# Reordered tokens in the slot strings of a causal convolution's product loop

## The chip, the cores and the metric

The kernel runs on one core of a Trainium2 chip. The metric is the device time of one execution in microseconds (us), the median over runs. The trace that goes with it is one profiled execution of the same program. The engines are called by the short names of the trace: PE (TensorE, matrix products), DVE (VectorE), ACT (ScalarE), POOL (GpSimd) and SP (SyncE, which here only issues transfers).

## The reference

```python
x:      (B=8, S=4096, D=512) float32
kernel: (K=8, 512, 512) float32
for k in range(8):
    shifted = x moved k places later along S (zeros come in, per batch)
    out += shifted @ kernel[k]
```

Each output row is the sum of eight products: the row itself and its seven predecessors, each with a 512x512 matrix of its own.

## The kernel before, in words

**Layout.** The 8 x 4096 rows are cut into 128 runs of 256 consecutive rows. One "time" t of all 128 runs is a block of 128 rows x 512. In `XR`, a ring of 20 such blocks in bf16, each block lies transposed (features on the partitions), so that it can be the stationary operand of a product. One `product` (line 116) is four matmuls, one for each 128 of the 512 features, accumulated into one PSUM bank of 128x512 float32.

**Fewer products.** The eight taps are split three times in two. At each split the kernel takes a sum or a difference of input blocks and of matrices, and so gets by with fewer products than the eight of the reference. Matrix sums are made once, at the start, into the tiles `W[a, b, c]`. Input sums are made all the time on DVE: `z` (line 137, differences or sums of blocks of `XR` into `Z`), `s` (line 151, pairs of `Z` into one of the two `S` tiles), `A` (line 148, pairs of `Z` into one of the two `A` tiles), and `F` in two halves (`node_F`, line 154: `F0` fills blocks 0 and 1 of the single tile `F`, `F1` blocks 2 and 3).

**Nodes and slots.** After a start that handles the first 16 times of each run (nodes 0 to 5, lines 331 to 561), 20 rounds follow, each for 12 new times. A round has four nodes, in the order PL, MI, H1, H0. The loop at line 569 handles one node for each pass, a slot. In a slot three nodes are worked on at once: `cur` gets its last products, `nxt` its middle ones, and `two` (two nodes ahead) has its input sums made. The string `SLOT[cur.a]` names the steps in the order in which they are issued. An engine carries out its own steps in that order; between engines only data dependencies count. This is all that sets the order: it is written by hand, and no planner moves anything.

The steps of a slot, each with its engine:

- `l00 l01 l10 l11`: products of `cur` (PE, line 210), one each into the four banks `p[b][:, j]`; they read block `2b+j` of `F`. For H0 each is two products that read `S`.
- `a1`/`b1`, `a0`, `u`: the products in the bank pair `q` of the node (PE, lines 164 to 182), with a copy by ACT between `a1` and the other two (lines 169, 172). `a1` and `a0` read `A`, `u` reads `Z`.
- `s0`, `s1`, `dt`: ACT copies that seed the bank pairs `p[0]`, `p[1]` of `nxt` from `q`, and the tile `DT` (lines 184, 192).
- `v0`, `v1`: products into `p[b][:, 1]` (PE). `d0`, `d1`: DVE makes `p[b][:, 0]` from `DT` and `p[b][:, 1]` (lines 205, 207). H0 has neither.
- `e0`, `e1`: the finished pair `p[b]` is taken out (line 233): by ACT for PL, by DVE for MI, H1 and H0; H1 and H0 then issue a store on SP. `g0`, `g1` (line 261): one more DVE combination each, and a store.
- `x`: SP issues DMA transposes of new blocks into `XR`, two in a PL slot and one in an MI slot, none in the others. They overwrite blocks that `z` has read.
- `r`: POOL copies two elements of `A` (line 107, so that it waits for `A`), then issues three loads of rows far ahead.

A step whose node lacks it issues nothing (`F`, `v`, `d`, `dt` of an H0 node).

The three bank pairs `pp0` to `pp2` go round from node to node; the fourth, `pp3`, is `q` of every node. So a seed waits until the pair's former node has been taken out.

Of the kernel before, what the change touches and what calls it, by code (L numbers as in the profile page):

```python
# [9 lines left out]
H1, H0, MI, PL = 0, 1, 2, 3  # L10
# [4 lines left out]
def kernel(  # L15
# [317 lines left out]
    for k in range(6):  # L333
# [227 lines left out]
    node_d(n6, 1)  # L561
    later = {6: ((H1, LO, MID),), 7: ((H1, HI, MID),)}
    SLOT = {
        PL: "s l00 F1 a0 l01 u l11 e0 s0 s1 dt F0 z x A v0 d0 v1 d1 l10 a1 e1",
        MI: "l00 s F1 a0 l01 u l11 e0 s0 s1 dt F0 z x A v0 d0 v1 d1 l10 a1 e1",
        H1: "l00 s F1 a0 l01 u l11 e0 s0 s1 dt F0 z A r g0 v0 d0 v1 d1 l10 e1",
        H0: "l00 s F1 b1 l01 a0 u l11 e0 s0 s1 dt F0 z x A g1 v0 d0 v1 d1 l10 a1 e1",
    }
    for k in range(6, len(nodes)):
        cur = nodes[k]  # L570
# [66 lines left out]
```

## Time and profile before

| | |
|---|---|
| runs | 759.54 us median of 3 (757.14 to 759.89) |
| profiled execution | 759.61 us, span 757.9 us |
| PE busy | 733.4 us of the span |
| DVE busy | 692.0 us of the span |
| ACT, POOL busy | 255.0, 62.1 us |
| start until 103 us | PE busy 9.43 of the first 15.40, 49.15 of the next 50.90, 28.02 of the next 36.70 |
| 103 to 133 us | PE busy 29.61, DVE busy 29.79 of 30.00 |
| 133 to 753 us | PE busy 616.87, DVE busy 595.06 of 620.00 |

The profiled execution's own time stands within 0.1 us of the median. Stamps below are us from the start of the span. A line of the timeline gives start, duration, engine, source line and operation, output and inputs, how many such instructions follow one another, and in brackets how long the engine had been idle and for whom it waited. The duration of a matmul reaches past the start of the next, since they overlap; the distance of starts is what one costs. The loop's first slot (PL) starts at 99.69 us on PE, and its first round ends at 133.19 us. All DVE additions and subtractions are issued from the one helper line L82; they are told apart by their tiles.

### The profile page before, as it was taken

To read this page: it belongs to the slowest core of one execution; us is meant where nothing else is said; L and a number is where in the kernel's file an instruction comes from. 1 tells how busy PE (TensorE), PEld (TensorE's weight loads), DVE (VectorE), ACT (ScalarE), POOL (GpSimd) and SP (SyncE) were. 2 spreads that over 40 slices of the span, in tenths; PEclk is the share of its full clock that TensorE was granted. 3 is DMA by queue.
4 is the path that set the end of the run, shared out by engine and by line. 5 is a ranking of instruction groups with operands and counts; after the bars stand their busy time and mean duration, and the time that the engine had idled before them with its cause. 6 is when DMAs were issued, how large, how long until landed. Compare 5 with 4: busy or idle time off the path is not lost.

```text
span 757.9 us, 8920 instructions
## 1 busy us (share of the span) xinstructions
PE 733.4 (97%) x3352; PEld 330.7 (44%) x3420; DVE 692.0 (91%) x727; ACT 255.0 (34%) x380; POOL 62.1 (8%) x103
## 2 busy tenths in 40 slices
PE   6999689999999999999999999999999999999997
PEld 2544234444444444444444444444444444444443
DVE  1774899999999999999999999999999999999996
ACT  4264332333333233333323333332423323232331
POOL 5020201010010101001010110101011010100000
PEclk9999899999999999999999999999999999999999
DMA  9979798877969688696977859597885958784424
GB/s 206 206 141 162 195 252 173 212 193 168 236 143 232 163 199 210 151 253 135 228 174 183 240 141 245 136 225 179 185 232 140 250 138 224 182 179 166 139 85 167
DMA packets 159948, 141.51 MB, mean 187 GB/s; under 512 B 130208, under 2 KB 134304, under 8 KB 159776
## 3 DMA queue, kind: packets, MB, share of 16 engines
q1 hardware_dynamic: 145456, 99.89, 47.0%
q0 software_dynamic: 14304, 40.77, 29.7%
q8 instruction: 27, 0.44, 0.2%
q10 hardware_dynamic: 144, 0.26, 0.1%
q14 instruction: 17, 0.14, 0.1%
HBM read 77.33 MB, written 98.57 MB: 232 GB/s over the span
## 4 chain that ended last, share of the span: by engine, by line
PE 88%; DVE 5%; DMA 4%; issue 1%; ACT 1%; POOL 0%; DVEq 0%; ACTq 0%; POOLq 0%
PE pp L118 87%; DMA w<-in_kernel_dram 2%; DMA out_dram<-w 1%; DMA XR<-xd 1%; DVE y L82 1%; DVE Z L82 1%; DVE S L82 1%; DVE w L82 1%; PE pp L295 0%; DVE F L82 0%; DVE pp L207 0%; PE pp L300 0%; DVE y L247 0%; DVE pp L82 0%; ACT pp L188 0%
## 5 line engine op out<-in xcount | busy, mean ns | idle before, releaser
L118 PE MATMUL pp<-w,S 128*128 128x512 bf16 x1114 | 261.6, 381 | 5.7 <-ACT pp L190 3.9
L118 PE MATMUL pp<-w,F 128*128 128x512 bf16 x973 | 248.4, 379 | 2.9 <-DVE pp L82 1.6
L118 PE MATMUL pp<-w,A 128*128 128x512 bf16 x668 | 173.1, 380 | 3.3 <-ACT pp L169 0.7
L118 PEld LDWEIGHTS <-S 128*128 128x128 bf16 x1136 | 111.1, 98 | 140.9 <-issue 9.5
L82 DVE TENSOR_TENSOR Z<-XR 128x3584 bf16<-128x3584 bf16 (+2 forms) x104 | 147.2, 1434 | 4.1 <-DMA XR<-xd 4.1
L118 PEld LDWEIGHTS <-F 128*128 128x128 bf16 x992 | 96.8, 98 | 119.4 <-issue 1.9
L82 DVE TENSOR_TENSOR S<-Z 128x2560 bf16<-128x2560 bf16 x80 | 118.6, 1483 | 0.0
L188 ACT COPY pp<-pp 128x1024 f32<-128x1024 f32 (+1 forms) x85 | 58.7, 691 | 157.6 <-PE pp L118 154.7
L118 PEld LDWEIGHTS <-A 128*128 128x128 bf16 x680 | 65.3, 98 | 87.2 <-DVE A L82 6.2
L172 ACT COPY pp<-pp 128x512 f32<-128x512 f32 x62 | 35.3, 570 | 201.6 <-PE pp L118 201.6
L118 PE MATMUL pp<-w,Z 128*128 128x512 bf16 x378 | 96.8, 379 | 1.1 <-DVE w L82 0.6
L82 DVE TENSOR_TENSOR F<-S 128x1024 bf16<-128x1024 bf16 x124 | 83.2, 684 | 0.0
L247 DVE SCALAR_TENSOR_TENSOR y<-pp,y 128x1024 f32<-128x1024 f32 x40 | 48.8, 1220 | 18.2 <-PE pp L118 17.2
L107 POOL COPY junk<-A 128x2 bf16<-128x2 bf16 x19 | 18.6, 979 | 540.9 <-DVE A L82 540.9
L190 ACT ACTIVATE pp<-pp 128x1024 f32<-128x1024 f32 (+1 forms) x85 | 59.5, 700 | 5.0 <-DVE y L82 3.8
L82 DVE TENSOR_TENSOR A<-Z 128x1024 bf16<-128x1024 bf16 x80 | 55.4, 692 | 3.9
L118 PEld LDWEIGHTS <-Z 128*128 128x128 bf16 x388 | 37.9, 98 | 46.5 <-issue 0.9
L82 DVE TENSOR_TENSOR y<-y,pp 128x1024 f32<-128x1024 f32 (+1 forms) x46 | 54.5, 1190 | 1.5 <-PE pp L118 1.5
L244 ACT ACTIVATE y<-pp 128x1024 f32<-128x1024 f32 x40 | 41.2, 1029 | 42.1 <-PE pp L118 42.1
L82 DVE TENSOR_TENSOR y<-pp,y 128x1024 f32<-128x1024 f32 x40 | 48.7, 1218 | 2.0 <-DMA out_dram<-y 2.0
L262 DVE SCALAR_TENSOR_TENSOR y<-y 128x1024 f32<-128x1024 f32 x40 | 48.7, 1218 | 0.0
L207 DVE SCALAR_TENSOR_TENSOR pp<-pp,DT 128x512 f32<-128x512 f32 x62 | 43.0, 693 | 2.8 <-PE pp L118 2.8
(53 smaller groups left out, 279.1 us busy)
## 6 DMA issues: line engine op xcount, KB each, us to landing
out_dram<-y SPq DMA_DIRECT2D x124, 512.0 KB, 7.8
xd<-in_x_dram POOLq DMA_DIRECT2D x60, 512.0 KB, 10.7
w<-in_kernel_dram POOLq DMA_DIRECT2D x8, 512.0 KB, 20.8
w<-w POOLq DMA_DIRECT2D x5, 512.0 KB, 6.8
w<-in_x_dram POOLq DMA_DIRECT2D x4, 512.0 KB, 11.7
out_dram<-w SPq DMA_DIRECT2D x3, 512.0 KB, 6.7
w<-in_x_dram SPq DMA_DIRECT2D x1, 1024.0 KB, 4.8
XR<-xd SPq DMA_TRANSPOSE x60, 5.1
```

What stands on the lines that cost most here:

```text
L82: nc.vector.tensor_tensor(out=o, in0=a, in1=b, op=op)
L107: nc.gpsimd.tensor_copy(out=junk, in_=z[:, 0:2])
L118: nc.tensor.matmul(bank, lhsT=comp[:, c * P:(c + 1) * P], rhs=w[:, c, :], start=start and c == 0, stop=c == DC - 1, skip_group_check=True)
L172: nc.scalar.copy(out=n.q[:, 0], in_=n.q[:, 1])
L188: nc.scalar.copy(out=o, in_=q)
L190: nc.scalar.mul(out=o, in_=q, mul=-1.0)
L207: nc.vector.scalar_tensor_tensor(out=p[:, 0], in0=p[:, 1], scalar=-1.0, in1=DT, op0=MUL, op1=SUB)
L244: nc.scalar.mul(out=cc[b_], in_=p, mul=0.5)
L247: nc.vector.scalar_tensor_tensor(out=dd[b_], in0=p, scalar=-0.5, in1=cc[b_], op0=MUL, op1=ADD)
L262: nc.vector.scalar_tensor_tensor(out=cc[b_], in0=cc[b_], scalar=2.0, in1=dd[b_], op0=MUL, op1=SUB)
```

## The change

Only the four strings change:

```diff
     SLOT = {
-        PL: "s l00 F1 a0 l01 u l11 e0 s0 s1 dt F0 z x A v0 d0 v1 d1 l10 a1 e1",
-        MI: "l00 s F1 a0 l01 u l11 e0 s0 s1 dt F0 z x A v0 d0 v1 d1 l10 a1 e1",
-        H1: "l00 s F1 a0 l01 u l11 e0 s0 s1 dt F0 z A r g0 v0 d0 v1 d1 l10 e1",
-        H0: "l00 s F1 b1 l01 a0 u l11 e0 s0 s1 dt F0 z x A g1 v0 d0 v1 d1 l10 a1 e1",
+        PL: "s l00 F1 a0 l01 u l11 e0 s0 z s1 v0 F0 A x dt d0 v1 d1 l10 a1 e1",
+        MI: "s l01 l00 F1 a0 u l11 e0 s0 z s1 dt A F0 v0 x v1 d1 l10 d0 e1 a1",
+        H1: "s l00 F1 a0 l01 u l11 s0 dt e0 z s1 A F0 g0 v0 d0 r v1 d1 l10 e1",
+        H0: "s l00 F1 b1 l01 a0 u e0 l11 s0 z s1 dt F0 A v0 x d0 g1 v1 d1 l10 a1 e1",
     }
```

No step is added or dropped, and no operand changes. What moves, read engine by engine (a step that issues nothing is left out):

| slot | engine | before | after |
|---|---|---|---|
| PL | DVE | s F1 F0 z A d0 d1 | s F1 z F0 A d0 d1 |
| MI | PE | l00 a0 l01 u l11 v0 v1 l10 a1 | l01 l00 a0 u l11 v0 v1 l10 a1 |
| MI | DVE | s F1 e0 F0 z A d0 d1 e1 | s F1 e0 z A F0 d1 d0 e1 |
| H1 | DVE | s F1 e0 z A g0 e1 | s F1 e0 z A g0 e1 |
| H0 | DVE | s e0 F0 z A g1 d0 d1 e1 | s e0 z F0 A d0 g1 d1 e1 |

PE's order in the other three slots, and the orders of ACT, SP and POOL in all four, are the same in both kernels: the second seed, `dt`, `x` and `r` move only past steps of other engines.

## The prediction

> **What bounds the kernel now.** I read the busy times first, then the chain that ended last.
>
> ```profile
> PE 733.4 (97%) x3352; PEld 330.7 (44%) x3420; DVE 692.0 (91%) x727; ACT 255.0 (34%) x380; POOL 62.1 (8%) x103
> ```
>
> PE and DVE are both nearly full, so either could bind. The chain in order of time (start, duration, what) tells when:
>
> ```profile
> 122.07 0.70 DVE A L82
> 122.82 2.78 PE pp L118 x12
> ...
> 133.19 10.79 PE pp L118 x49
> 143.98 0.05 issue
> 144.03 10.78 PE pp L118 x49
> ```
>
> Up to the first round of the loop the chain runs through DVE; from 133 us on it is PE alone, matmul after matmul, until 753 us. A round is 152 matmuls and 32.90 us (l00 of PL starts at 133.19 and, nine rounds later, at 429.33): 20 rounds. Within one steady round, the four slots PL, MI, H1, H0 (each engine's busy us, then granted clock, DMA share, GB/s):
>
> ```profile
> 396.43:404.22 7.79, 7.74 (x36) 3.48 (x36) 7.69 (x9) 3.09 (x5) 0.00 (x0) 1.00 1.01 300
> 404.22:412.01 7.79, 7.79 (x37) 3.51 (x36) 6.73 (x9) 3.09 (x5) 0.00 (x0) 1.00 0.71 138
> 412.01:417.22 5.21, 5.16 (x25) 2.34 (x24) 5.21 (x6) 2.11 (x3) 0.00 (x0) 1.00 0.44 105
> 417.22:429.33 12.11, 12.06 (x57) 5.41 (x56) 12.04 (x14) 2.54 (x5) 2.52 (x4) 1.00 0.80 196
> ```
>
> The third number group is DVE: full but for 1.06 us in MI. So PE binds, DVE has one gap for each round, and what DVE makes arrives shortly before PE needs it. The MI slot shows the gap:
>
> ```profile
> 404.22 1.03 PE L118 MATMUL pp<-w,F 128*128 128x512 bf16 x4
> 405.10 1.02 PE L118 MATMUL pp<-w,A 128*128 128x512 bf16 x4
> 405.96 1.03 PE L118 MATMUL pp<-w,F 128*128 128x512 bf16 x4
> 406.82 1.03 PE L118 MATMUL pp<-w,Z 128*128 128x512 bf16 x4
> 407.02 1.23 DVE L247 SCALAR_TENSOR_TENSOR y<-pp,y 128x1024 f32<-128x1024 f32 x1 [1.02 <-PE pp L118]
> 410.29 1.03 PE L118 MATMUL pp<-w,F 128*128 128x512 bf16 x4
> 410.63 0.69 DVE L82 TENSOR_TENSOR pp<-DT,pp 128x512 f32<-128x512 f32 x1
> 411.22 0.69 DVE L207 SCALAR_TENSOR_TENSOR pp<-pp,DT 128x512 f32<-128x512 f32 x1
> 412.01 1.03 PE L118 MATMUL pp<-w,F 128*128 128x512 bf16 x4
> ```
>
> That is l00, a0, l01, u, then e0 (which waits for l01, 0.20 after u starts), l10, d0, d1, and l00 of H1, which needs d0.
>
> **The change part by part.** Nothing is added or removed; every instruction keeps its duration. The question is only which arrival becomes late for PE, or early enough to remove a wait.
>
> *MI, a0 behind both l's.* a0 waits for the ACT copy behind a1 (404.48 for 0.57, so 405.05). The step from l00 to a0 is 0.88 us, the others 0.86. With l01 in between, the copy has 0.86 more: 0.02 x 20 rounds = 0.4 us less. The bounds are 0 and, by two-digit stamps, 0.03 x 20 = 0.6. H1 keeps l00 a0 (412.01 to 412.90, 0.89) and its wait.
>
> *MI, e0.* Both l's are done one product earlier: e0 can start at 405.96 + 0.20 = 406.16, not 407.02. DVE then has s and F1 done (405.92), so most of the 1.02 gap closes, and z, A, F0 follow by their spacings (1.13, 1.25, 0.61, 0.60) until 409.75.
>
> *MI, d1 before d0.* This opens a new wait. d1 needs v1, the product just ahead of l10. How long after l10's start? e0 gives 0.20; nearer is another d1 that waited for its v1, at the start:
>
> ```profile
> 67.82 1.89 PE L118 MATMUL pp<-w,S 128*128 128x512 bf16 x8
> 68.96 0.70 DVE L207 SCALAR_TENSOR_TENSOR pp<-pp,DT 128x512 f32<-128x512 f32 x1 [2.77 <-PE pp L118]
> ```
>
> Eight matmuls are v1 and v0; v0 starts 0.86 in, at 68.68, and d1 0.28 later. I take 0.28, the same operation: d1 at 410.57, d0 at 411.17, done at 411.86. PE waited for d0 once at the start (done 99.64, matmul 99.69), so 0.05 more: 411.91, against 412.01. The margin falls from 0.64 to 0.10 (0.18 with 0.20). Cost nothing, by that margin; each 0.1 us beyond it costs 20 x 0.1 = 2 us. Behind d0 on DVE stand e1 (411.77, before 411.82), s of H0, F1, e0 of H1 (414.90; it needs l01, 414.63 + 0.20), z and A of PL, done by 418.85 instead of 418.90. PE's b1 needs that A at 418.96, the tightest arrival of the round, and it gains 0.05.
>
> *PL and H0, z before F0.* F0 ends some 2 us later: in PL at 402.1, for l01 of MI at 404.22; in H0 at about 426.1, for l00 of PL at 429.33. Covered by 2.1 and 3.2 us. z and A were neighbours, and A starts 0.03 to 0.10 after z ends (z 399.99 for 2.02, A 402.11), while unrelated neighbours start 0.08 before the end. F0 in between takes that out: 0.11 to 0.18 of DVE in each of the two slots. In steady rounds PE does not notice.
>
> [...]
>
> *H0, d0 before g1.* d0 comes 1.4 us earlier, v0 permitting (v1 starts at 425.88, so from 426.16); l00 of PL had 0.5 us left and has more. g1 and its store come 0.6 later; on SP only e1's store stands behind it, two us away.
>
> *First round, where DVE binds.* PE waits there once for A of PL (0.16 at 122.82). d0 of MI in its new place: z to F0 to A of PL gains 0.18, so d1 starts at 114.37 and d0 ends at 115.66 against 115.24; l00 of H1 wanted 115.54 and starts at 115.71, 0.17 late. But A of PL, DVE 0.18 ahead, ends at 122.58 instead of 122.76, and PE, 0.17 late, arrives at 122.66: in all 0.16 earlier.
>
> *SP, POOL, ACT.* Transposes in PL start 0.6 earlier with z (402.03 before, landing 6.1 later, read at 416.09), the one in MI up to 1.4 earlier; the next store on SP is at 416.20. POOL waits for the same A as before. ACT's seeds wait for u, unmoved; s1 of H1 waits for e0, now earlier.
>
> Sum: -0.4 - 0.16 = -0.56. On the profiled execution, 759.61 (1.7 around the 757.9 span), that is 759.05; its own time is 0.07 above the median of the runs, so I say 759.0. No measurement here tells changes under 0.5% (3.8 us, 0.19 a round) from none.
>
> **Rivals.**
>
> *d0 becomes the bound (slower).* If d1 is released by the end of the next product, l10, and not of v1, it starts at 411.15 + 0.28 = 411.43 and d0 reaches PE at 412.77, 0.76 late: 20 x 0.76 = 15 us, 774. Against it: 68.96, where d1 went while v0 ran. For it: nothing but the thin margin. It decides from 0.10 + 0.19 = 0.29 us of extra delay in each round.
>
> *A smaller form of it.* PE loads weights ahead of a matmul, at 411.80 here. If d0 had to be there for the load, it is 0.11 late, 2.2 us: 761; with a release worse by another 0.1, 763.2. Against it: at 97.67 a load ran two us ahead of the matmul that waited until 99.69.
>
> *PE gets denser (faster).* In the row of 24 matmuls of the H0 slot (423.29 to 428.46) one costs 0.2154; 152 of them are 32.74, 0.16 less than the round. If earlier arrivals removed all of that, 19 x 0.16 = 3.1 us: 755.9. Against it: the other products keep their 0.86 where nothing is late. For more there is no idle time on PE.
>
> The Trainium skill, "TensorE: Matmul & The Clock Gate", section "Back-to-back issue gap", gives about 131 ns for a matmul of 512 columns in a sustained stream. The trace has 0.2165 us. By the page PE would need 20 us a round, DVE with 31.7 would bind, and its savings of up to 0.36 a round would come out as 20 x 0.36 = 7.2 us, 752.3.
>
> **How the numbers follow.** Forecast (no new wait, 758.3 to 759.9): 0.64. Denser PE: 0.14, of which about half beyond 3.8 us, if the runs fall on the low side like 757.14. Small wait: 0.08. d0 bound: 0.11. Unseen others: 0.03. So faster 0.07, same 0.79, slower 0.14. The range takes in the denser PE below (755.9) and the small wait above (763.2); it leaves out the d0 bound and a part of the denser PE.
>
> **What the new profile would show.** In MI, L247's first wait shrinks from 1.02 to about 0.2 and a wait of about 0.8 appears ahead of L207 (d1). Right: round of 32.9 us, l00 of H1 0.86 after a1, a0 of MI no more than 0.87 after its neighbour. Wrong: PE waits named for DVE pp at l00 of H1, 20 times; or a round clearly off 32.9 us.

## The result and the profile after

| | before | after |
|---|---|---|
| runs beside each other (6 each) | 758.92 us median (757.14 to 759.89) | 756.76 us (755.24 to 759.11) |
| ratio | | 0.9979, 95% interval 0.9955 to 1.0003 |
| once more (23 and 12 runs) | 758.45 us (755.27 to 760.16) | 757.57 us (754.77 to 759.43) |
| ratio | | 0.9990, 0.9970 to 1.0009 |
| span of the profiled execution | 757.9 us | 757.3 us |

Both intervals contain 1: the runs do not tell the two kernels apart. The two profiled executions do. Both reach the loop's first product at the same stamp (99.69 and 99.70 us), so their stamps can be compared directly.

The page after (busy us, share of the span, instructions):

```profile
PE 733.1 (97%) x3352; PEld 331.8 (44%) x3420; DVE 690.1 (91%) x727; ACT 254.9 (34%) x380; POOL 62.0 (8%) x103
```

The same work, on the same engines. The chain that ended last, after:

```profile
102.77 0.61 DVE F L82
103.39 0.05 issue
103.43 7.73 PE pp L118 x35
111.16 0.05 issue
111.21 10.91 PE pp L118 x49
122.12 0.05 issue
122.17 10.77 PE pp L118 x49
```

It turns from DVE to PE at 103 us, not only at 133. The wait of b1 for A is nearly gone: b1 starts 1.74 us after l00 of H0 (120.88 to 122.62), where the kernel before has 2.06 (120.76 to 122.82) and a steady round 1.73. The chain hides one wait of that round, because the duration of the product ahead reaches past it: l00 of H1 waits for d0 and starts at 115.70, 1.02 after a1 (114.68) instead of 0.86. The four slots of one steady round after, in the columns shown for before:

```profile
396.08:403.90 7.82, 7.77 (x37) 3.49 (x37) 7.82 (x9) 3.09 (x5) 0.00 (x0) 1.00 1.16 300
403.90:411.68 7.78, 7.78 (x38) 3.52 (x37) 6.50 (x9) 3.09 (x5) 0.00 (x0) 1.00 0.89 165
411.68:416.88 5.20, 5.15 (x24) 2.34 (x24) 5.20 (x6) 2.11 (x3) 0.00 (x0) 1.00 0.24 62
416.88:428.97 12.09, 12.04 (x57) 5.45 (x56) 12.06 (x14) 2.55 (x5) 2.52 (x4) 1.00 0.81 194
```

The round is 32.89 us instead of 32.90. DVE's gap in MI is 1.28 instead of 1.06, and PE is as full as before. The MI slot of that round, PE and DVE:

```profile
403.90 1.89 PE L118 MATMUL pp<-w,F 128*128 128x512 bf16 x8
405.62 1.03 PE L118 MATMUL pp<-w,A 128*128 128x512 bf16 x4
405.82 1.23 DVE L247 SCALAR_TENSOR_TENSOR y<-pp,y 128x1024 f32<-128x1024 f32 x1 [0.54 <-PE pp L118]
...
409.95 1.03 PE L118 MATMUL pp<-w,F 128*128 128x512 bf16 x4
410.22 0.70 DVE L207 SCALAR_TENSOR_TENSOR pp<-pp,DT 128x512 f32<-128x512 f32 x1 [0.71 <-PE pp L118]
410.81 1.03 PE L118 MATMUL pp<-w,Z 128*128 128x512 bf16 x4
410.83 0.69 DVE L82 TENSOR_TENSOR pp<-DT,pp 128x512 f32<-128x512 f32 x1
411.42 1.22 DVE L247 SCALAR_TENSOR_TENSOR y<-pp,y 128x1024 f32<-128x1024 f32 x1
411.68 0.59 PE L118 MATMUL pp<-w,F 128*128 128x512 bf16 x2
```

The new wait of d1 for v1 is there (0.71). d1 starts 0.27 after l10 does (410.22 - 409.95), d0 ends at 411.52, and l00 of H1 starts at 411.68, 0.87 after a1: d0 is in time, by about 0.1 us.

### The profile page after: what moved, and what is told of

Its sections match the earlier page's. It is cut to its first block, busy times and chain, and to the rows that moved or that the text cites. A ratio compares the mean times of both kernels' runs of the same rounds, so it can differ in the third digit from the quotient of the medians.

```text
span 757.3 us, 8900 instructions
## 1 busy us (share of the span) xinstructions
PE 733.1 (97%) x3352; PEld 331.8 (44%) x3420; DVE 690.1 (91%) x727; ACT 254.9 (34%) x380; POOL 62.0 (8%) x103
## 4 chain that ended last, share of the span: by engine, by line
PE 91%; DMA 4%; DVE 2%; issue 1%; ACT 0%; POOL 0%; DVEq 0%; ACTq 0%; POOLq 0%
PE pp L118 91%; DMA w<-in_kernel_dram 2%; DMA out_dram<-w 1%; DMA XR<-xd 1%; DVE y L82 1%; DVE w L82 1%; PE pp L295 0%; DVE S L82 0%; PE pp L300 0%; ACT pp L188 0%; DVE Z L82 0%; DVE F L82 0%; ACT pp L169 0%; ACT pp L190 0%; DVE pp L82 0%
## 5 line engine op out<-in xcount | busy, mean ns | idle before, releaser
L118 PE MATMUL pp<-w,F 128*128 128x512 bf16 x973 | 245.3, 379 | 2.9 <-DVE pp L82 1.7
```

Source lines behind the costliest of these rows:

```text
L118: nc.tensor.matmul(bank, lhsT=comp[:, c * P:(c + 1) * P], rhs=w[:, c, :], start=start and c == 0, stop=c == DC - 1, skip_group_check=True)
```

## A measure that leaves the start out

The runs of one kernel spread over some 5 us, ten times what is at stake. The profiled executions show where most of that lies, ahead of the loop: its first product starts anywhere from 95.80 to 99.83 us, in kernels whose code up to there is the same. So each kernel is read by two numbers that do not contain the start: the time from the loop's first product to the start of the last group on DVE (e1 of the last H0 slot), and the length of a steady round, the distance of the same product row over 15 to 18 rounds. "Alone" means that only this part of the change was made, in the kernel before.

| kernel | loop starts | last DVE group | between | steady round |
|---|---|---|---|---|
| before | 99.69 | 753.42 | 653.73 | 32.904 |
| after | 99.70 | 752.91 | 653.21 | 32.886 |
| after, second execution | 97.46 | 750.76 | 653.30 | 32.89 |
| PE's order in MI alone | 99.69 | 753.08 | 653.39 | 32.885 |
| z and A earlier alone | 97.70 | 751.26 | 653.56 | 32.905 |
| d1 ahead of d0 alone | 95.80 | 749.54 | 653.74 | 32.905 |
| F0 between d1 and d0 | 97.70 | 761.15 | 663.45 | 33.41 |
| d0 behind e1 | 99.83 | 776.71 | 676.88 | 34.07 |
| a0 ahead of both l's | 97.54 | 768.25 | 670.71 | 33.771 |
| swap in PL and H1 too | 97.35 | 749.24 | 651.89 | 32.816 |

The two executions of the changed kernel differ by 0.09 us in this measure and by 0.004 in the round, so it tells some tenths of a microsecond, and not hundredths. The three kernels with one part alone, the one with d0 behind e1 and the one with a0 ahead were each executed once. The whole times of the three are 759.27, 757.46 and 755.75 us in the order of the table, beside 757.13 for one execution of the kernel before; they follow the loop's start (99.69, 97.70 and 95.80) and say nothing of the parts.

## The experiments

**The changed kernel again**, no edit.

> The changed kernel once more, beside the kernel before on the same chip. Theory 1 (PE arrivals: the round is 32.887 us instead of 32.904, and the first round 0.2 us shorter; nothing else differs): 0.55 us below the kernel before, ratio 0.9993, in the profile and in the runs; the further 1.6 us by which the medians of the result differ come from the granted clock of the single runs. Theory 2 (the freed wait of DVE lets something outside the rounds end earlier too): 2.2 us below, ratio 0.9971.

Measured: ratio 0.9990 (0.9970 to 1.0009). From the loop's start, 653.30 us: 0.43 below the kernel before, where the first execution had 0.52. Theory 1 holds for what the loop does. Its last clause, that the granted clock of the single runs makes the rest, is not shown; the last section takes it up. The interval still reaches to 0.9971, so the runs alone do not exclude theory 2; the loop's time does not show a gain of 2.2, and neither does the end (the last product, then DVE, is the same in both).

**PE's order in MI alone.**

```diff
-        MI: "l00 s F1 a0 l01 u l11 e0 s0 s1 dt F0 z x A v0 d0 v1 d1 l10 a1 e1",
+        MI: "l01 l00 s F1 a0 u l11 e0 s0 s1 dt F0 z x A v0 d0 v1 d1 l10 a1 e1",
```

> The kernel before with the new order of PE in MI alone (l01 l00 a0 u). Theory 1 (the shorter round comes from a0, which no longer waits for ACT's copy): round 32.887 instead of 32.904, 19 or 20 x 0.017 = 0.3 us less; the first wait of e0 in MI falls from 1.02 to some 0.2. Theory 2 (it comes from the order on DVE): round stays 32.904.

Measured: round 32.885, 0.34 us less from the loop's start. The whole shortening of the round comes from this part, but only about half of it is the wait of a0 that theory 1 names. In the kernel before, the rounds are not alike: of the 18 behind the first, seven take 32.915 to 32.920 us and eleven 32.893 to 32.897 (l00 of H1 starts at 379.12, 412.01 and 444.93). Here all 18 take 32.884 to 32.887. The seven are the rounds in which the blocks for z of PL wrap round the ring `XR`, so that z is two instructions. In the kernel before, z, A and then b1, first in a short round and then in a long one:

```profile
383.20 2.02 DVE L82 TENSOR_TENSOR Z<-XR 128x3584 bf16<-128x3584 bf16 x1
385.25 0.69 DVE L82 TENSOR_TENSOR A<-Z 128x1024 bf16<-128x1024 bf16 x1
386.05 1.03 PE L118 MATMUL pp<-w,A 128*128 128x512 bf16 x4
...
416.09 2.08 DVE L82 TENSOR_TENSOR Z<-XR 128x1536 bf16<-128x1536 bf16 x2
418.21 0.69 DVE L82 TENSOR_TENSOR A<-Z 128x1024 bf16<-128x1024 bf16 x1
418.96 1.04 PE L118 MATMUL pp<-w,A 128*128 128x512 bf16 x4
```

A ends 0.11 us before b1 starts in the short round and 0.06 before it in the long one. 0.06 is also the distance in the first round, where PE waited for A (122.76 to 122.82), so in the long rounds b1 is late and waits for DVE. With l01 ahead, e0 in MI starts about a product earlier, A of PL comes 0.12 earlier against PE, and that wait is gone. Counted by rounds, the seven waits of 0.024 are about 0.16 us, and a0 gives about 0.009 a round, 0.16 us in all. The smaller figure is only twice the 0.004 by which the two executions of the changed kernel differ.

**z and A earlier alone** (and nothing else).

```diff
-        PL: "... s0 s1 dt F0 z x A v0 d0 ...",
+        PL: "... s0 s1 dt z F0 x A v0 d0 ...",
-        MI: "... s0 s1 dt F0 z x A v0 d0 ...",
+        MI: "... s0 s1 dt z x A F0 v0 d0 ...",
-        H0: "... s0 s1 dt F0 z x A g1 ...",
+        H0: "... s0 s1 dt z F0 x A g1 ...",
```

> The kernel before with z and A ahead of F0 on DVE in PL, MI and H0 as in the changed kernel (PL and H0: z F0 A; MI: z A F0), PE's order and d0, d1, g1 as before. Theory 1: in the first round A of PL comes 0.18 earlier, at 122.64 for b1 instead of 122.82, and PE, not held up by d0, is 0.18 ahead from there on; the round stays 32.904; in all -0.2 us. Theory 2 (DVE pays a pipeline flush after every operation whatever stands next): A of PL at 122.82 as before, 0.

Measured: round 32.905, 0.17 us less from the loop's start. In the first round, l00 of H0 and then b1 on PE:

```profile
118.75 1.89 PE L118 MATMUL pp<-w,S 128*128 128x512 bf16 x7
120.63 1.04 PE L118 MATMUL pp<-w,A 128*128 128x512 bf16 x4
```

1.88 us lie between the two, where the kernel before has 2.06 (120.76 to 122.82). A of PL comes 0.18 sooner, once, as theory 1 has it.

**d1 ahead of d0 alone.**

```diff
-        MI: "... A v0 d0 v1 d1 l10 a1 e1",
+        MI: "... A v0 v1 d1 l10 d0 a1 e1",
```

> The kernel before with d1 ahead of d0 in MI alone. Theory 1: first round l00 of H1 0.35 late (115.89 instead of 115.54), of which 0.02 is left at b1 (DVE is late there anyway); steady rounds d0 ends at 411.92 and reaches PE at 411.97, against 412.01: no wait, round 32.904. So 0. Theory 2 (the wait for v1 comes later than taken, or d0 has to be there for the weight load 0.21 ahead of the matmul): 0.05 to 0.2 in each round, 1 to 4 us.

Measured: round 32.905, 0.01 us more from the loop's start. In the first round PE waits for d0, here with its line:

```profile
112.00 1.02 PE L118 MATMUL pp<-w,F 128*128 128x512 bf16 x4 [0.18 <-DVE pp L82]
```

This row starts 1.21 after the product before it (110.79) instead of 0.86, so l00 is 0.35 late; a part of that is not counted as idle because a matmul's duration reaches past the next start. At b1 the loss is gone, since A is late there anyway. The forecast loss and its return are both there.

**The margin of d0, first step: F0 between d1 and d0.** Edit on the changed kernel:

```diff
-        MI: "s l01 l00 F1 a0 u l11 e0 s0 z s1 dt A F0 v0 x v1 d1 l10 d0 e1 a1",
+        MI: "s l01 l00 F1 a0 u l11 e0 s0 z s1 dt A v0 x v1 d1 F0 l10 d0 e1 a1",
```

> The changed kernel with F0 of MI moved between d1 and d0, so that d0 stands 0.60 us later on DVE. Theory 1 (d0 releases l00 of H1 and its margin is 0.11: done 411.52 in the changed profile, 0.05 to the matmul, which starts at 411.68): l00 of H1 is 0.49 late in each round, 20 x 0.49 = 9.8 us, about 768. Theory 2 (d0 stands off PE's path, or PE has room elsewhere in the round to make it up): no change.

Measured: 768.15 us, ratio to the kernel before 1.0137 (1.0109 to 1.0164); from the loop's start 10.24 us more than the changed kernel. A steady round on PE, a1, l00 of H1, and further on l00 of H0 and b1:

```profile
413.34 1.03 PE L118 MATMUL pp<-w,Z 128*128 128x512 bf16 x4
414.70 1.02 PE L118 MATMUL pp<-w,F 128*128 128x512 bf16 x4 [0.33 <-DVE pp L82]
...
419.87 1.89 PE L118 MATMUL pp<-w,S 128*128 128x512 bf16 x8
421.69 1.04 PE L118 MATMUL pp<-w,A 128*128 128x512 bf16 x4
```

l00 starts 1.36 after a1 instead of 0.87, 0.49 late. That is the 0.60 by which d0 was pushed back, less a margin of 0.11. A second, smaller loss was not forecast: b1 is 0.09 late here (1.82 instead of 1.73), because A of PL stands behind d0 on DVE. This is one of the long rounds, in which z is two instructions; in the others b1 is 0.02 late, some 0.05 in the mean. A third entry gives back 0.03: a0 of H1, which follows l00, has no wait left. Together about 0.51 a round, where the rounds differ by 0.52 (33.41 - 32.89).

**The margin, second step: d0 behind e1.** On the changed kernel:

```diff
-        MI: "... v0 x v1 d1 l10 d0 e1 a1",
+        MI: "... v0 x v1 d1 l10 e1 d0 a1",
```

> The changed kernel with d0 of MI moved behind e1. e1 needs l10, so it starts 0.20 after a1's first matmul (410.81, so 411.01), d0 1.14 later at 412.15, done at 412.84, and l00 of H1 at 412.89 instead of 411.68. Theory 1: 1.21 us late in each round, 20 x 1.21 = 24 us, about 783. Theory 2 (d0 off the path): no change.

Measured, in one execution: 782.91 us; from the loop's start 23.67 us more than the changed kernel, 1.19 a round. A steady round, e1, d0 and l00 of H1:

```profile
421.75 1.23 DVE L247 SCALAR_TENSOR_TENSOR y<-pp,y 128x1024 f32<-128x1024 f32 x1
422.89 0.69 DVE L82 TENSOR_TENSOR pp<-DT,pp 128x512 f32<-128x512 f32 x1
423.63 1.02 PE L118 MATMUL pp<-w,F 128*128 128x512 bf16 x4 [1.05 <-DVE pp L82]
```

d0 ends at 423.58 and the matmul starts 0.05 later. Theory 2 of both steps falls: but for the 0.03 at a0 of H1, the round has no room that makes up for a late d0.

**a0 ahead of both l's.** On the kernel before:

```diff
-        MI: "l00 s F1 a0 l01 u ...",
+        MI: "s a0 l00 F1 l01 u ...",
```

> The kernel before with a0 of MI ahead of l00 too, so that no product stands between a1 and a0. Theory 1 (a0 is paced by ACT's copy behind a1, which reaches PE 0.88 us after the next product could start; one product between them costs 0.86 and so hides all but 0.02, two hide it whole): l00 comes 0.88 late, the round is 32.90 - 0.02 + 0.88 = 33.76, 20 x 0.86 = 17 us more, about 776. Theory 2 (the 0.88 is how these two products are spaced, and no wait): round 32.90.

Measured, in one execution: 774.45 us, round 33.771, 16.98 us more from the loop's start. a1 and a0 of that round:

```profile
408.65 1.03 PE L118 MATMUL pp<-w,A 128*128 128x512 bf16 x4
410.39 1.02 PE L118 MATMUL pp<-w,A 128*128 128x512 bf16 x4 [0.71 <-ACT pp L172]
```

From the start of a1 to the start of a0 at least 1.74 us pass, by way of ACT. One product between them takes the step to 0.86 + 0.88 = 1.74 as well, so it did not hide the copy whole. Two hide it with room: in the changed kernel a0 starts 2.59 after a1 (403.03 to 405.62). That is the wait taken as 0.02.

**The swap in PL and H1 too.** On the changed kernel:

```diff
-        PL: "s l00 F1 a0 l01 u l11 ...",
+        PL: "s l01 l00 F1 a0 u l11 ...",
-        H1: "s l00 F1 a0 l01 u l11 ...",
+        H1: "s l01 l00 F1 a0 u l11 ...",
```

> The changed kernel, and PL and H1 too issue l01 l00 a0 u instead of l00 a0 l01 u. Theory 1 (a0 waits some 0.02 to 0.03 us for ACT's copy wherever only one product stands between a1 and a0; in PL the copy-out e0 on ACT also holds up the seed for v0 by 0.03): H1 gains 0.03, PL 0.01 at a0 and 0.03 at v0, so the round falls from 32.887 to 32.82, 20 x 0.07 = 1.4 us less than the changed kernel. Theory 2 (the 0.88 steps are how matmuls are spaced and no wait): no change against the changed kernel.

Measured: 754.67 us median of 12 runs (753.42 to 756.66), ratio to the kernel before 0.9962 (0.9946 to 0.9979); round 32.816, 1.32 us less than the changed kernel from the loop's start. PL of one round, from l01 and l00 to v0 and v1:

```profile
426.00 1.89 PE L118 MATMUL pp<-w,F 128*128 128x512 bf16 x8
427.72 1.03 PE L118 MATMUL pp<-w,A 128*128 128x512 bf16 x4
428.58 1.03 PE L118 MATMUL pp<-w,Z 128*128 128x512 bf16 x4
429.45 1.03 PE L118 MATMUL pp<-w,F 128*128 128x512 bf16 x4
430.31 1.89 PE L118 MATMUL pp<-w,S 128*128 128x512 bf16 x8
```

and the same stretch of the kernel before, from u on:

```profile
431.93 1.03 PE L118 MATMUL pp<-w,Z 128*128 128x512 bf16 x4
432.79 1.03 PE L118 MATMUL pp<-w,F 128*128 128x512 bf16 x4
433.69 1.02 PE L118 MATMUL pp<-w,S 128*128 128x512 bf16 x4
```

l11 to v0 is 0.86 instead of 0.90: ACT takes out e0 a product earlier and is free when the seed for v0 can be made (e0 at 427.92, the seed at 429.65 after 0.70 of idle time; before, e0 at 432.13 and the seed at 433.05 right behind it). This is the one kernel here whose interval lies wholly below 1, and by the loop's time it beats both the kernel before and the changed one. The loop accounts for 1.84 us of the 3.8 by which its runs lie below the kernel before. That is a ratio of 0.9976, inside the interval; what the runs show beyond it the loop does not explain.

## Why the prediction was right, point by point

- *What bounds.* PE from the second round of the loop on, with DVE's deliveries just ahead of it. Shown: with d0 0.60 and 1.33 later against PE (its end 1.57 after l10's start in the changed kernel, 2.90 with d0 behind e1), l00 was 0.49 and 1.21 late.
- *a0 behind both l's, -0.4.* This part alone gave -0.34, but the agreement is in part luck. That a0 waits for the copy was read from a step of 0.88 against 0.86, and it is so: with a0 first it is a wait of 0.71 in the trace, and with two products between there is no wait. Its size was taken too large, 0.02 a round from two-digit stamps, where about 0.009 came out, 0.16 us in all. As much again came from a wait at which the prediction looked and put no price: it called A of PL for b1 "the tightest arrival of the round", with A done at 418.90 and b1 at 418.96, and took b1 as in time. It was 0.024 us late in each of the seven long rounds.
- *First round, -0.16.* Measured -0.17 for z ahead of F0 alone, and 0.20 earlier for l00 of the second round in the whole change (132.99 instead of 133.19). The steps came as worked out: d1 at 114.36 (114.37 forecast), l00 of H1 at 115.70 (115.71), b1 at 122.62 (122.66). Only at b1 it was not PE that came last, as worked out, but A, by 0.02.
- *d1 before d0, nothing.* Measured 0.01 alone. The margin was put at 0.10 by the slower of two rows and 0.18 by the faster; the slower was right (0.27 from l10 to d1), and the margin found by pushing d0 is 0.11. The 0.05 that A of PL was to gain did not come: in this kernel alone A still ends 0.06 before b1 in the long rounds.
- *Sum, -0.56.* The parts alone give -0.34 - 0.17 + 0.01 = -0.50, the whole change -0.52 and in its second execution -0.43, the span -0.6.
- *A flush of DVE after every operation* (theory 2 of "z and A earlier alone"). The rows decide against it here: in the changed PL slot z starts at 398.87 and takes 2.01, F0 starts at 400.80, 0.08 before z ends, and A after F0 likewise.
- *Two sizes that were off.* e0's wait in MI was to shrink to about 0.2; it is 0.54. The order of PE alone does bring it to 0.27; z and A earlier alone lengthen it from 1.02 to 1.34, since without the bubbles of PL and H0 DVE reaches e0 some 0.3 earlier, which the step on e0 had left out. It costs nothing, since e0 still waits for PE. And d1's wait was to be about 0.8; it is 0.71.
- *The time itself.* 759.0 was forecast and 756.76 measured, with 755.9 to 763.2 as the range. Most of this distance is no part of the change: the median of the kernel before went from 759.54 (3 runs) to 758.92 (6 runs), and from there the forecast would read 758.4. The other 1.6 us the loop does not show; the start, which no edit touches, spreads over 4 us. The forecast took no account of that beyond the three runs shown. That the median still fell inside the range, 0.9 us from its end, is luck too.
- *Rivals.* d0 as the bound: not in the changed kernel, and true as soon as d0 stands 0.11 us later. The weight load: excluded, since the load for l00 ran from 411.46 on, before d0 ended at 411.52, and l00 was on time. Denser PE: excluded for this change (0.018 a round, not 0.16); the swap in all three slots finds 0.088 of those 0.16. A matmul in some 0.131 us: not seen; the densest round here, 32.816 us, is 0.2159 for each of its 152.

## What to carry to other kernels

On an engine that is full, look for steps between instructions that are a few hundredths longer than their neighbours: they can be waits too short for a table of waits, and a product moved in between can remove them. Compare single rounds before taking a mean: a wait that comes in two rounds of five hides in it, and its gain is then put down to something else. Before an operation is put behind a later-arriving one on another engine's queue, work out its margin from the rows and expect to pay all that exceeds it, once in every round. Where runs spread more than a change can bring, take a measure that leaves the noisy stretch out, such as the length of a steady round.

## What the hardware showed that was not expected

The start of the kernel, untouched by any edit, ends anywhere between 95.80 and 99.83 us. PE's matmuls before and after a wait there for ACT (line 190), in the changed kernel, in the same kernel in its second execution, and in the kernel with d1 ahead of d0 alone:

```profile
77.10 0.81 PE L118 MATMUL pp<-w,XR 128*128 128x512 bf16 x3 [0.42 <-ACT DT L194]
81.77 3.57 PE L118 MATMUL pp<-w,S 128*128 128x512 bf16 x8 [3.86 <-ACT pp L190]
85.13 1.91 PE L118 MATMUL pp<-w,A 128*128 128x512 bf16 x4
```

```profile
75.57 0.81 PE L118 MATMUL pp<-w,XR 128*128 128x512 bf16 x3 [0.41 <-ACT DT L194]
79.54 2.93 PE L118 MATMUL pp<-w,S 128*128 128x512 bf16 x8 [3.16 <-ACT pp L190]
82.27 1.71 PE L118 MATMUL pp<-w,A 128*128 128x512 bf16 x4
```

```profile
75.81 0.81 PE L118 MATMUL pp<-w,XR 128*128 128x512 bf16 x3 [0.41 <-ACT DT L194]
77.93 1.89 PE L118 MATMUL pp<-w,S 128*128 128x512 bf16 x8 [1.30 <-ACT pp L190]
79.65 1.03 PE L118 MATMUL pp<-w,A 128*128 128x512 bf16 x4
```

After a wait of 3.86 us the eight matmuls take 3.36 us to the next start (0.42 each), after 3.16 us 2.73, after 1.30 us 1.72 (0.215 each). The granted clock between 80 and 90 us is 0.66, 0.83 and 1.00. The Trainium skill, "TensorE: Matmul & The Clock Gate", section "Part 1: The HAM clock gate (the "warmup" mystery)", says that PE falls to half its clock after an idle window of about 3.4 us, of a monitor that runs freely. The rates agree (0.42 and 0.215 us), but a shorter wait was enough here: in the kernel with a0 first, eight matmuls after a wait of 2.96 us took 3.36 us, all at half rate.

The lower clock goes with a late loop, but it does not make it late. From the first matmul after the wait to the loop's first product 17.93, 17.92 and 17.87 us pass, after the slow matmuls as after the fast ones (17.87 to 18.30 in all ten executions). What differs is when the wait ends, at 81.77, 79.54 and 77.93, and with it the loop starts at 99.70, 97.46 and 95.80. Both come behind the transposes in front of them on the chain, which took 8.99, 8.29 and 6.42 us: the DVE sum `Z` behind them starts at 75.43, 73.20 and 71.58, and the loop 24.27, 24.26 and 24.22 us later (24.2 to 24.7 in all ten executions). Why the same transposes take longer in one execution than in another was not tried. No edit here touched that stretch; it moves the time by more than everything in the loop that was tried for a gain.
